# First four value blocks of the gMLP layer computed side by side in four PSUM banks, feature row by feature row; x loaded in eight pieces

## The chip, the cores and the metric

The kernel runs on one core of a Trainium2 chip. Its time is that of one execution on the device, in microseconds (us); lower is better. The engines named below are TensorE (PE; its weight loads are listed as PEld), VectorE (DVE), ScalarE (ACT), GpSimd (POOL) and SyncE (SP), which here only issues DMA loads and stores.

## What is computed

One inference step of a two-layer decoder trunk on 320 tokens at once: 256 of a prompt and 8 x 8 of a sample group. Model width is 1024. Layer 0 mixes tokens with a gated MLP over chunks of 128, layer 1 with an mLSTM; each is followed by a gated MLP with a causal convolution. The change lies in the first matrix product of layer 0, `x @ w_in`, and in what stands around it:

```python
h = rmsnorm(x, norm_mix_g[0])
h = jax.nn.gelu(h @ w_in)                 # 1024 -> 4096
u, v = jnp.split(h, 2, axis=-1)           # 2048 each
v = (v - mu) * rsqrt(var + EPS) * ln_g + ln_b
mixed = einsum('gts,bnsgd->bntgd', tril(w_s), v) + b_s
x = x + (u * mixed) @ w_out
```

## The kernel before

**Layout.** x is kept transposed: `xT` holds 8 feature rows (KD) of 128 features by T = 320 tokens. Weights lie in memory in blocks of 128 output features; a block of `a_win` is 128 x 8 x 128 floats, 512 KB: 8 feature rows of 64 KB. Blocks 0 to 15 give u, blocks 16 to 31 give v; the v blocks come first.

**Precision.** Every f32 product is made of three fast ones. `norm_block` (L163, L164) writes x times the norm's gain as a high half `xh` (ACT) and a low half `xl` (DVE); `prefetch` does the same with weights: `wh` (ACT, L124) and `wl` (DVE, L125). `chunk` then issues, for each feature row k, wh.xh, wh.xl and wl.xh into one PSUM accumulator: 3 matmuls of 128 x 128 by 320 columns a row, 24 a block. The root mean square itself is not applied to x: it enters later, by token, as the scale `rc` of the gelu, or as the row `rb`.

**Queues of weights.** `weights` writes the list of loads for the whole kernel, in the order of use. `prefetch(n, m)` issues loads on SP up to entry n and splits up to entry m. Four `raw` buffers hold loaded entries: a load waits until the split of the entry four places before it is done. `wh` and `wl` have three buffers each: a split waits until PE has finished with the entry three before. `take` hands the next entry to PE, keeping loads 4 entries and splits 1 entry ahead (AHEAD, SPLIT_AHEAD).

**Order.** All PE instructions keep the order in which the program writes them (`pin`). The other engines' queues are ordered by the framework's scheduler when the kernel is built, by priority and by the time at which it reckons each instruction ready; each queue then runs strictly in that order, waiting where it must. Buffers of a pool are handed out by the same scheduler.

**The start.** `run` issues ten warm-up matmuls of `ones` into a PSUM bank `pw`, then loads the first 16 columns of `vecs`, and in four steps two feature rows of x (320 KB) and one entry of weights, with `norm_block` and the weight split behind each. The first block (16) is listed in pieces of 2, 2 and 4 feature rows, the second (17) in two of 4, the others whole. `ident` and the rest of `vecs` are loaded last.

**Layer A.** In the first loop of `layer_a`, over the 16 v blocks, `block` makes one block in one of three `pm` banks of PSUM, DVE copies it to SBUF (`vT`, L289), and one loop pass later `v_nat` turns it by three PE transposes to tokens by features, into banks `pvt`. Four blocks share three `pvt` banks; after the fourth, ACT takes the gelu of each with scale `rc` (L269) and DVE its statistics (L270). Between the blocks stand, each at a fixed loop pass: the squares of x (`square_block`, b = 1: ACT squares, DVE adds to `acc`), `norm_cols` (b = 3: six small matmuls into a bank `pc`; then `ms` on DVE, L193, and `rc` on POOL, L196), `load_ws` (b = 3: loads of the spatial weights, masked by `trit` on POOL, L251), `norm_row` (b = 5: `dg`, `pb`, `rb`) and `row_sums` (b = 10). `pw`, `pvt`, `pc`, `pb` and others share the five `pa` banks; PSUM has eight banks in all.

A second loop makes the u blocks, and what follows in the kernel is not touched by the change.

Of the kernel before, what the change touches and what calls it, by code (L numbers as in the profile page):

```python
# [10 lines left out]
F32 = mybir.dt.float32  # L11
# [5 lines left out]
P = 128  # L17
# [3 lines left out]
T = TP + NB * NS  # L21
D = 1024
KD = D // P
# [10 lines left out]
V_MIX, V_FFN, V_FIN, V_GN, V_LG, V_LB, V_CB, V_FB, V_FW, V_CW = 0, 16, 32, 40, 56, 72, 88, 104, 148, 280  # L34
# [3 lines left out]
class Net:  # L38
# [19 lines left out]
    def weights(self):  # L58

        I = self.I  # L60
        q = []

        def add(w, b, *groups, k0=0):
            for kn in groups:
                q.append((w, b, k0, kn))
                k0 += kn

        add(I["a_win"], 16, 2, 2, 4)
        add(I["a_win"], 17, 4, 4)
        for b in [*range(18, 32), *range(16)]:  # L70
            add(I["a_win"], b, 8)
        for b in range(KD):
            add(I["a_wo"], b, 8, 8)

        def ffn(l):
            for b in range(2 * KF):
                add(I["f_up"][l], b, 8)
            for b in range(KD):
                add(I["f_dn"][l], b, 8, 7, 7)

        ffn(0)
        add(I["b_wg"], 0, 8)
        for h in range(NH):
            for r in range(6):
                if (h, r) == (NH - 1, 4):
                    for b in (0, 1):
                        add(I["b_wo"], b, 6, k0=8)
                add(I["b_win"], 6 * h + r, 8)
                for b in self.EARLY_OUT.get((h, r), ()):
                    add(I["b_wo"], b, 8)  # L90
        for b in range(KD):
            if b < 2:
                add(I["b_wo"], b, 2, k0=14)
            else:
                add(I["b_wo"], b, 8, k0=8)
        ffn(1)
        self.wq = q
        self.loaded, self.halved, self.used = [], [], 0
# [37 lines left out]
    def chunk(self, ps, rhs, first, last):  # L136
        (wh, wl), kn = self.take()
        for k in range(kn):
            xh, xl = rhs(k)
            self.mm(ps[:, :T], wh[:, k, :], xh, first and k == 0, False)  # L140
            self.mm(ps[:, :T], wh[:, k, :], xl, False, False)
            self.mm(ps[:, :T], wl[:, k, :], xh, False, last and k == kn - 1)

    def block(self, kt, rhs):

        ps = self.psm.tile([P, 512], F32, tag="pm", name="pm")
        done = 0
        while done < kt:
            kn = self.wq[self.used][3]
            self.chunk(ps, lambda k: rhs(done + k), done == 0, done + kn == kt)  # L150
            done += kn
        return ps
# [75 lines left out]
    def layer_a(self):  # L228
        nc, tc, I, O = self.nc, self.tc, self.I, self.O
        with tc.tile_pool(name="ya", bufs=1) as yp, tc.tile_pool(name="la", bufs=1) as lp:  # L230
# [13 lines left out]
            def load_ws():  # L244
                nc.sync.dma_start(ws, I["a_ws"])
                nc.sync.dma_start(trit, I["trit"])
                nc.gpsimd.memset(wss[:64], 0.0)
                nc.sync.dma_start(wss[64:], I["a_wss"])
                nc.sync.dma_start(bdt[64:], I["bdt"])
                nc.sync.dma_start(bs, I["a_bs"].to_broadcast([P, NH, P]))  # L250
                nc.gpsimd.tensor_tensor(ws, ws, trit.unsqueeze(1).to_broadcast([P, NH, P]), op=MULT)  # L251
                nc.gpsimd.tensor_tensor(wss[64:], wss[64:], bdt[64:].unsqueeze(1).to_broadcast([64, NH, 64]), op=MULT)

            def row_sums():
                for i in range(2):
                    pr = self.psa.tile([P, 512], F32, tag="pa", name="pr")
                    self.mm(pr, self.ones, ws[:, 4 * i:4 * i + 4, :], True, True)
                    nc.scalar.copy(rsum[:, 4 * i:4 * i + 4, :].rearrange("p g t -> p (g t)"), pr)

            def v_nat(b, vT):  # L260
                q, c = b // 4, b % 4
                if c == 0:
                    pvt[q] = [self.psa.tile([P, 512], F32, tag="pa", name="pvt") for _ in range(3)]
                for t in range(3):
                    self.tr(pvt[q][t][:, c * P:(c + 1) * P], self.tokens(vT, t), self.ident)
                if c == 3:
                    for t in range(3):
                        vv = v[:, t, q * 512:(q + 1) * 512]
                        nc.scalar.activation(vv, pvt[q][t], AF.Gelu_apprx_tanh, scale=self.rc[:, t:t + 1])  # L269
                        nc.vector.bn_stats(st[:, t, q, :], vv)  # L270

            prev = None
            for b in range(16):
                ps = self.block(KD, self.x_rhs)
                if b == 1:
                    with tc.issue_after(self.last_split.ins):
                        for m in range(KD):
                            self.square_block(m)
                if b == 3:
                    self.norm_cols()  # L280
                    load_ws()
                if b == 5:
                    self.norm_row()
                if b == 10:
                    row_sums()
                if prev is not None:
                    v_nat(b - 1, prev)
                prev = lp.tile([P, T], F32, tag="vT", name="vT", bufs=2)
                nc.vector.tensor_copy(prev, ps[:, :T])  # L289

            ve = lp.tile([P, 3], F32, name="ve_a")
            rs = lp.tile([P, 3], F32, name="rstd_a")
# [45 lines left out]
            for b in range(16):  # L338
                ps = self.block(KD, self.x_rhs)
# [586 lines left out]
    def run(self):  # L926
        nc, tc, I, O = self.nc, self.tc, self.I, self.O
        with tc.tile_pool(name="const", bufs=1) as cp, tc.tile_pool(name="xp", bufs=1) as xp, \
                tc.tile_pool(name="wraw", bufs=4) as wraw, tc.tile_pool(name="wsp", bufs=3) as wsp, \
                tc.tile_pool(name="tp", bufs=2) as tp, \  # L930
                tc.tile_pool(name="psm", bufs=3, space=bass.MemoryType.PSUM) as psm, \
                tc.tile_pool(name="psa", bufs=5, space=bass.MemoryType.PSUM) as psa:
            self.wraw, self.wsp, self.tp, self.psm, self.psa = wraw, wsp, tp, psm, psa
            self.xT = xp.tile([P, KD, T], F32, name="xT")
            self.xh = xp.tile([P, KD, T], F32R, name="xh")
            self.xl = xp.tile([P, KD, T], F32R, name="xl")
            self.vecs = cp.tile([P, NVEC], F32, name="vecs")
            self.ident = cp.tile([P, P], F32, name="ident")
            self.ones = cp.tile([P, P], F32, name="ones")
            self.mhalf = cp.tile([P, 1], F32, name="mhalf")  # L940
            self.weights()
            nc.vector.memset(self.mhalf, -0.5)
            warm = cp.tile([P, 1], F32, name="warm")
            nc.scalar.activation(warm, self.mhalf, AF.Gelu_apprx_tanh)
            nc.vector.memset(self.ones, 1.0)
            pw = psa.tile([P, 512], F32, tag="pa", name="pw")
            for i in range(10):
                self.mm(pw[:, :P], self.ones, self.ones, True, True)
            nc.sync.dma_start(self.vecs[:, :16], I["vecs"][:, :16])
            for i in range(4):  # L950
                nc.sync.dma_start(self.xT[:, 2 * i:2 * i + 2, :], I["xT"][:, 2 * i:2 * i + 2, :])
                self.prefetch(i + 1, 0)
                for m in (2 * i, 2 * i + 1):
                    self.norm_block(m, V_MIX)
                self.prefetch(i + 1, min(i + 1, 3))
            nc.sync.dma_start(self.ident, I["ident"])
            nc.sync.dma_start(self.vecs[:, 16:], I["vecs"][:, 16:])
            self.layer_a()
            self.ffn(0, V_MIX + 8)
            self.layer_b()  # L960
            self.ffn(1, None)


def _blocks(w, order=None):

    K, N = w.shape
    b = w.reshape(K // P, P, N // P, P).transpose(2, 1, 0, 3)
    return np.ascontiguousarray(b if order is None else b[order])
# [7 lines left out]
def _lay_out(i):  # L976
    a = {}
    x = np.concatenate([i["x_prompt"].reshape(TP, D), i["x_sample"].reshape(NB * NS, D)])
# [2 lines left out]
        [_cols(i[n]) for n in ("norm_mix_g", "norm_ffn_g", "final_norm_g", "b_gn_g", "a_ln_g", "a_ln_b", "b_conv_b", "f_conv_b",  # L981
                               "f_conv_w", "b_conv_w")], axis=1))
    a["a_win"] = _blocks(i["a_w_in"][0])
    a["a_wo"] = _blocks(i["a_w_out"][0])
    ws = i["a_w_s"][0]
    a["a_ws"] = np.ascontiguousarray(ws.transpose(2, 0, 1))
# [13 lines left out]
    w = i["b_w_in"][0]  # L1000
# [63 lines left out]
```

## Time and profile before

| | |
|---|---|
| median of 3 runs | 982.02 us (981.94 to 982.76) |
| the profiled execution | 981.71 us |
| its span, first to last instruction | 980.0 us |
| granted TensorE clock, mean | 0.996 |
| moved by DMA | 154.63 MB, 158 GB/s over the span |

The profile records one execution. Its views list busy time of each engine, the chain of work that ended last, groups of equal instructions, the waits, the DMA transfers and a timeline of each engine. In a timeline row the columns are the start and duration in us, the engine, the line of the kernel, the operation, what it writes and reads, the tile's size and type, and the number of instructions merged; in brackets stand the idle time of that engine just before it and what ended it. Matmuls overlap in the pipeline, so a matmul's recorded duration is longer than the distance to the next one.

### The profile page before, as it was taken

The page shows a single profiled execution, that of the slowest core. Times are in us where ns is not written, and L with a number is a line of the kernel's source. Part 1 is how long each engine was busy: PE and PEld are TensorE (multiplying, and loading weights), DVE is VectorE, ACT ScalarE, POOL GpSimd, SP SyncE. Part 2 cuts the span into 40 slices and gives each one's busy share as a digit, 9 for nine tenths or more (in the row PEclk, how much of TensorE's full clock was granted, in tenths as well). Part 3 has the DMA queues.
Part 4 walks back from the last instruction along what each step waited for, and adds up shares of the span by engine and source line. Part 5 has one row for each costly group of instructions (what it writes and reads, how often), then busy time and mean ns, then how long its engine had stood idle before and what let it go on. Part 6 is the DMA issues. An engine that isn't in the chain of part 4 may idle for free.

```text
span 980.0 us, 17587 instructions
## 1 busy us (share of the span) xinstructions
PE 966.2 (99%) x6695; PEld 959.7 (98%) x6695; DVE 700.6 (71%) x1358; ACT 510.4 (52%) x918; POOL 95.4 (10%) x266
## 2 busy tenths in 40 slices
PE   9999999999999999999999999999999999999996
PEld 8999999999999999999999999999999999999996
DVE  6647985577777764559999988787787777775442
ACT  6437444454544543349676765565555455544332
POOL 0100000010000000013231111111101000000000
PEclk9999999999999999999999999999999999999998
DMA  8535434444444455455565664553364444445541
GB/s 281 199 129 152 131 136 150 150 151 151 151 144 156 143 154 143 153 174 169 167 214 165 202 199 157 173 175 136 129 210 139 152 151 151 151 145 150 154 119 54
DMA packets 55958, 154.63 MB, mean 158 GB/s; under 512 B 6610, under 2 KB 17490, under 8 KB 55874
## 3 DMA queue, kind: packets, MB, share of 16 engines
q1 hardware_dynamic: 55874, 153.51, 48.1%
q8 instruction: 53, 0.87, 0.4%
q14 instruction: 31, 0.25, 0.1%
HBM read 141.55 MB, written 11.94 MB: 157 GB/s over the span
## 4 chain that ended last, share of the span: by engine, by line
PE 83%; issue 10%; DVE 4%; ACT 2%; DMA 1%; SPq 0%; POOL 0%; POOLq 0%; DVEq 0%; ACTq 0%
PE pm L47 75%; PE num L47 2%; PE pcs L47 1%; PE pmix L47 1%; DVE wl L125 1%; DVE bcv L601 1%; PE pvt L50 1%; DMA xT<-in_xT 0%; ACT wh L124 0%; PE pv L50 0%; PE psc L47 0%; PE pCp L47 0%; PE phn L50 0%; DMA C<-in_C 0%; PE pg L47 0%
## 5 line engine op out<-in xcount | busy, mean ns | idle before, releaser
L124 ACT CAST wh<-raw 128x1024 fp32r<-128x1024 f32 (+3 forms) x253 | 257.3, 1018 | 355.0 <-PE pm L47 197.2
L47 PE MATMUL pm<-xh,wh 128*128 128x320 f32 x1344 | 419.3, 312 | 1.0 <-ACT wh L124 1.0
L47 PE MATMUL pm<-xh,wl 128*128 128x320 f32 x1344 | 415.9, 309 | 1.9 <-DVE wl L125 1.7
L47 PE MATMUL pm<-xl,wh 128*128 128x320 f32 x1344 | 415.1, 309 | 0.0
L125 DVE TENSOR_TENSOR wl<-raw,wh 128x1024 fp32r<-128x1024 f32 (+3 forms) x253 | 299.6, 1185 | 117.4 <-ACT wh L124 114.8
L47 PEld LDWEIGHTS pm<-xh,wl 128*128 128x128 f32 x1344 | 252.2, 188 | 3.2 <-DVE wl L125 3.2
L47 PEld LDWEIGHTS pm<-xh,wh 128*128 128x128 f32 x1344 | 252.5, 188 | 1.9 <-ACT wh L124 1.5
L47 PEld LDWEIGHTS pm<-xl,wh 128*128 128x128 f32 x1344 | 252.5, 188 | 0.2
L47 PE MATMUL pm<-yh_f,wh 128*128 128x320 f32 x352 | 109.0, 310 | 0.0
L47 PE MATMUL pm<-yh_f,wl 128*128 128x320 f32 x352 | 108.5, 308 | 0.0
L47 PE MATMUL pm<-yl_f,wh 128*128 128x320 f32 x352 | 108.5, 308 | 0.0
L47 PEld LDWEIGHTS pm<-yl_f,wh 128*128 128x128 f32 x352 | 66.1, 188 | 0.0
L47 PEld LDWEIGHTS pm<-yh_f,wh 128*128 128x128 f32 x352 | 66.1, 188 | 0.0
L47 PEld LDWEIGHTS pm<-yh_f,wl 128*128 128x128 f32 x352 | 66.1, 188 | 0.0
L393 DVE SCALAR_TENSOR_TENSOR fcv<-fpad,vecs,fcv 128x336 f32<-128x336 f32 x88 | 49.6, 566 | 2.1 <-ACT fcv L391 0.7
L216 DVE TENSOR_TENSOR xT<-pm,xT 128x320 f32<-128x320 f32 x40 | 19.5, 490 | 41.9 <-PE pm L47 41.9
L47 PE MATMUL pm<-ylb,wh 128*128 128x320 f32 x128 | 39.9, 312 | 0.5 <-DVE ylb L815 0.4
L47 PE MATMUL pm<-yhb,wh 128*128 128x320 f32 x128 | 40.0, 312 | 0.4 <-ACT yhb L814 0.4
L47 PE MATMUL pm<-yhb,wl 128*128 128x320 f32 x128 | 39.6, 309 | 0.0
L47 PE MATMUL pm<-yh_a,wh 128*128 128x320 f32 x128 | 39.6, 309 | 0.0
L47 PE MATMUL pm<-yh_a,wl 128*128 128x320 f32 x128 | 39.5, 308 | 0.0
L47 PE MATMUL pm<-yl_a,wh 128*128 128x320 f32 x128 | 39.5, 308 | 0.0
(254 smaller groups left out, 1262.6 us busy)
## 6 DMA issues: line engine op xcount, KB each, us to landing
raw<-in_f_up SPq DMA_DIRECT2D x88, 512.0 KB, 3.3
raw<-in_b_win SPq DMA_DIRECT2D x48, 512.0 KB, 3.4
raw<-in_a_win SPq DMA_DIRECT2D x30, 512.0 KB, 3.7
raw<-in_f_dn SPq DMA_DIRECT2D x32, 448.0 KB, 3.3
C<-in_C SPq DMA_DIRECT2D x32, 258.0 KB, 3.7
raw<-in_a_wo SPq DMA_DIRECT2D x16, 512.0 KB, 3.7
raw<-in_f_dn SPq DMA_DIRECT2D x16, 512.0 KB, 3.5
out_Cs<-C SPq DMA_DIRECT2D x32, 256.0 KB, 2.7
```

Of the source, the lines that this page charges most:

```text
L47: self.pin(self.nc.tensor.matmul(out, lhsT, rhs, start=start, stop=stop))
L50: self.pin(self.nc.tensor.transpose(out, in_, ident))
L124: self.last_split = nc.scalar.copy(wh[:, :kn, :], raw[:, :kn, :])
L125: nc.vector.tensor_tensor(wl[:, :kn, :], raw[:, :kn, :], wh[:, :kn, :].bitcast(F32), op=SUB)
L216: self.nc.vector.tensor_tensor(x, ps[:, :T], x, op=ADD)
L393: nc.vector.scalar_tensor_tensor(cv, pd[:, i:i + NC], self.vec(w + i * KF), cv, op0=MULT, op1=ADD)
L601: nc.vector.scalar_tensor_tensor(cv, pd[:, i:i + NC], self.vec(w + 16 * i), cv, op0=MULT, op1=ADD)
```

## The change

- A second copy of the weights of blocks 16 to 19 is laid out by feature row (`a_w4`): entry k is the four blocks' share of feature row k, 256 KB. The weight list begins with these eight entries in place of blocks 16 to 19 (the first two of which came in five pieces).
- `first` makes the four blocks together. It takes three `pm` banks and one `pa` bank, and for each feature row issues 12 matmuls: wh.xh into each of the four banks, then wh.xl, then wl.xh.
- x is loaded one feature row at a time (160 KB). `run` issues the loads of rows 0 to 3, each followed by a weight entry, and the splits of row 0; `first` issues the others, one in each of its passes, and `norm_block` for the row after the one in work.
- The warm-up has eight matmuls instead of ten.
- After `first`, the four accumulators are copied out (`v_copy`); there are four `vT` buffers instead of two. The loop begins at block 4. The squares move from b = 1 to 4, `norm_cols` and `load_ws` from 3 to 6, `norm_row` from 5 to 8, `row_sums` from 10 to 11. The transposes of blocks 0 to 6 are done two, one, two and two at passes 4, 5, 6 and 7; from pass 8 on one block behind, as before.

```diff
--- before.py
+++ after.py
@@ -65,9 +65,9 @@
                 q.append((w, b, k0, kn))
                 k0 += kn
 
-        add(I["a_win"], 16, 2, 2, 4)
-        add(I["a_win"], 17, 4, 4)
-        for b in [*range(18, 32), *range(16)]:
+        for k in range(KD):
+            add(I["a_w4"], k, 4)
+        for b in [*range(20, 32), *range(16)]:
             add(I["a_win"], b, 8)
         for b in range(KD):
             add(I["a_wo"], b, 8, 8)
@@ -141,6 +141,25 @@
             self.mm(ps[:, :T], wh[:, k, :], xl, False, False)
             self.mm(ps[:, :T], wl[:, k, :], xh, False, last and k == kn - 1)
 
+    def load_x(self, k):
+        self.nc.sync.dma_start(self.xT[:, k, :], self.I["xT"][:, k, :])
+
+    def first(self):
+
+        ps = [self.psm.tile([P, 512], F32, tag="pm", name="pm") for _ in range(3)]
+        ps.append(self.psa.tile([P, 512], F32, tag="pa", name="pm"))
+        for k in range(KD):
+            if k + 4 < KD:
+                self.load_x(k + 4)
+            if k + 1 < KD:
+                self.norm_block(k + 1, V_MIX)
+            (wh, wl), _ = self.take()
+            xh, xl = self.x_rhs(k)
+            for w, x, a, z in ((wh, xh, k == 0, False), (wh, xl, False, False), (wl, xh, False, k == KD - 1)):
+                for j in range(4):
+                    self.mm(ps[j][:, :T], w[:, j, :], x, a, z)
+        return ps
+
     def block(self, kt, rhs):
 
         ps = self.psm.tile([P, 512], F32, tag="pm", name="pm")
@@ -269,24 +288,29 @@
                         nc.scalar.activation(vv, pvt[q][t], AF.Gelu_apprx_tanh, scale=self.rc[:, t:t + 1])
                         nc.vector.bn_stats(st[:, t, q, :], vv)
 
-            prev = None
-            for b in range(16):
+            def v_copy(ps):
+                vT = lp.tile([P, T], F32, tag="vT", name="vT", bufs=4)
+                nc.vector.tensor_copy(vT, ps[:, :T])
+                return vT
+
+            vTs = {b: v_copy(ps) for b, ps in enumerate(self.first())}
+            for b in range(4, 16):
                 ps = self.block(KD, self.x_rhs)
-                if b == 1:
+                if b == 4:
                     with tc.issue_after(self.last_split.ins):
                         for m in range(KD):
                             self.square_block(m)
-                if b == 3:
+                if b == 6:
                     self.norm_cols()
                     load_ws()
-                if b == 5:
+                if b == 8:
                     self.norm_row()
-                if b == 10:
+                if b == 11:
                     row_sums()
-                if prev is not None:
-                    v_nat(b - 1, prev)
-                prev = lp.tile([P, T], F32, tag="vT", name="vT", bufs=2)
-                nc.vector.tensor_copy(prev, ps[:, :T])
+                for m in {4: (0, 1), 5: (2,), 6: (3, 4), 7: (5, 6)}.get(b, (b - 1,)):
+                    v_nat(m, vTs.pop(m))
+                vTs[b] = v_copy(ps)
+            prev = vTs.pop(15)
 
             ve = lp.tile([P, 3], F32, name="ve_a")
             rs = lp.tile([P, 3], F32, name="rstd_a")
@@ -944,15 +968,15 @@
             nc.scalar.activation(warm, self.mhalf, AF.Gelu_apprx_tanh)
             nc.vector.memset(self.ones, 1.0)
             pw = psa.tile([P, 512], F32, tag="pa", name="pw")
-            for i in range(10):
+            for i in range(8):
                 self.mm(pw[:, :P], self.ones, self.ones, True, True)
             nc.sync.dma_start(self.vecs[:, :16], I["vecs"][:, :16])
-            for i in range(4):
-                nc.sync.dma_start(self.xT[:, 2 * i:2 * i + 2, :], I["xT"][:, 2 * i:2 * i + 2, :])
-                self.prefetch(i + 1, 0)
-                for m in (2 * i, 2 * i + 1):
-                    self.norm_block(m, V_MIX)
-                self.prefetch(i + 1, min(i + 1, 3))
+            for k in range(4):
+                self.load_x(k)
+                self.prefetch(k + 1, 0)
+                if k == 0:
+                    self.norm_block(0, V_MIX)
+                    self.prefetch(1, 1)
             nc.sync.dma_start(self.ident, I["ident"])
             nc.sync.dma_start(self.vecs[:, 16:], I["vecs"][:, 16:])
             self.layer_a()
@@ -981,6 +1005,7 @@
         [_cols(i[n]) for n in ("norm_mix_g", "norm_ffn_g", "final_norm_g", "b_gn_g", "a_ln_g", "a_ln_b", "b_conv_b", "f_conv_b",
                                "f_conv_w", "b_conv_w")], axis=1))
     a["a_win"] = _blocks(i["a_w_in"][0])
+    a["a_w4"] = np.ascontiguousarray(a["a_win"][16:20].transpose(2, 1, 0, 3))
     a["a_wo"] = _blocks(i["a_w_out"][0])
     ws = i["a_w_s"][0]
     a["a_ws"] = np.ascontiguousarray(ws.transpose(2, 0, 1))
```

## The prediction

> **What bounds the kernel now.** I read the page first, then busy time by stretch, then the chain of waits in order of time, then the engines' own timelines up to 35 us.
>
> ```profile
> span 980.0 us, 17587 instructions
> PE 966.2 (99%) x6695; PEld 959.7 (98%) x6695; DVE 700.6 (71%) x1358; ACT 510.4 (52%) x918; POOL 95.4 (10%) x266
> ```
>
> ```profile
> 1.00:10.33 9.33, 7.88 (x34) 6.43 (x35) 4.50 (x11) 6.08 (x13) 0.32 (x1) 1.00 0.84 280
> 10.33:120.00 109.67, 109.67 (x765) 108.36 (x766) 79.72 (x140) 58.71 (x86) 6.74 (x4) 1.00 0.54 175
> ```
>
> In the second fence the columns are the stretch, its length, then busy time of PE, PEld, DVE, ACT and POOL, the granted clock, the DMA share and GB/s. TensorE works without a gap from 10.33 us through the whole of layer A; only before 10.33 does it stand still. So whatever the change does is decided on PE's own timeline: what it saves ahead of 10.33, less every new gap.
>
> ```profile
> 3.14 4.86 DMA xT<-in_xT
> ...
> 9.64 0.65 DVE wl L125
> ...
> 10.33 5.25 PE pm L47 x34
> 15.58 0.33 PE pvt L50 x3
> 15.91 3.52 PE pm L47 x24
> 19.43 0.33 PE pvt L50 x3
> 19.76 3.51 PE pm L47 x24
> 23.27 0.56 PE pc L47 x6
> ```
>
> This is the chain of waits in order of time. The start hangs on the load of x and the splits behind it; after 10.33 everything on the chain is PE. A block of 24 matmuls takes 3.51 us, 0.146 each, and a value block's three transposes 0.33. From 10.33 to 23.27 PE issues 82 of the first four blocks' 96 matmuls, so 14 were done before. Without the two groups of transposes the four blocks end at 23.27 - 0.66 = 22.61 us: the number to compare with.
>
> ```profile
> 1.16 4.64 PE L47 MATMUL pw<-ones 128*128 128x128 f32 x20 [1.16 <-DVE ones L945]
> 5.65 0.43 PE L47 MATMUL pm<-xh,wh 128*128 128x320 f32 x1
> 5.92 0.31 PE L47 MATMUL pm<-xl,wh 128*128 128x320 f32 x1
> ```
>
> On PE's timeline the warm-up ends at 5.80 and the first real matmul starts at 5.65. After an idle time the second matmul comes 0.27 after the first instead of 0.146: each restart costs another 0.12. Fourteen matmuls are 2.05 us of work, spread over 4.68 us (5.65 to 10.33): about 2.6 us are lost in gaps, and this is the most the change can take away, beyond what an earlier first matmul brings.
>
> **The front, with feature rows.** A row now gives PE 12 matmuls, 12 x 0.146 = 1.75 us, for 160 KB of x and 256 KB of weights. When these land I take from the first uses in the profile.
>
> ```profile
> 4.29 1.01 ACT L163 ACTIVATE xh<-xT,vecs 128x320 fp32r<-128x320 f32 x2 [1.99 <-DMA xT<-in_xT]
> ...
> 6.30 1.02 ACT L163 ACTIVATE xh<-xT,vecs 128x320 fp32r<-128x320 f32 x2 [0.70 <-DMA xT<-in_xT]
> ...
> 8.03 1.01 ACT L163 ACTIVATE xh<-xT,vecs 128x320 fp32r<-128x320 f32 x2 [0.42 <-DMA xT<-in_xT]
> 8.95 0.60 ACT L124 CAST wh<-raw 128x512 fp32r<-128x512 f32 x1
> ...
> 11.73 0.62 ACT L124 CAST wh<-raw 128x512 fp32r<-128x512 f32 x1 [0.53 <-DMA raw<-in_a_win]
> ```
>
> Four of these waited for a load, so they date a sum of KB in the order of issue (8 of vecs, then x and weights in turn; before the last also ident and the rest of vecs): 328 KB at 4.29, 776 at 6.30, 1224 at 8.03, 2540 at 11.73. That is 223, 259 and 356 KB per us. In the new order the sum is 168 after x row 0, 424 after its weights, 840 after row 1, 1256 after row 2, 1672 after row 3. Interpolated, they land at 3.6, 4.7, 6.55, 8.1 and 9.3 us. SP issues them at 0.43 and a little each, eight from 1.26 to about 5.0, as before:
>
> ```profile
> 1.72 0.43 SPq L109 DMA_DIRECT2D raw<-in_a_win  x1
> ```
>
> A row's cast is the 128x512 form, 0.60, so the casts of rows 0 to 3 end near 5.3, 7.15, 8.7 and 9.9. On ACT a row costs 0.60 + about 0.5 (half of the 1.01), and DVE's two splits come to about 1.2 by the rows below; both stay under PE's 1.75. PE starts row 0 at 5.37, row 1 at 7.25 (its cast is just done), and from there each row 1.75 later: 9.0, 10.75, 12.5. The later rows lead by more and more.
>
> x rows 4 to 7 are moved: they now stand on SP behind ident and vecs, and each after the first also behind a weight load that waits for a buffer (four raw buffers; load k+4 waits for row k's split). Load 4 waits for the first split, near 6.0, lands at a sum of 2316 KB, 11.1, and its cast ends at 11.7, needed at 12.5. Load 5 waits for split 1, near 8.0, and lands by its sum, 2732 KB, at 12.3; its cast ends at 12.9, needed at 14.25. Loads 6 and 7 have over 1 us too. So no row starves: 96 x 0.146 + 0.12 behind 5.37 ends the four blocks near 19.6, with 0.1 lost before row 1. Gain: 22.61 - 19.6 = **3.0 us**. Bounds: row 0's 424 KB lie between 328 KB (4.29) and 776 KB (6.30), so the gain lies between 3.4 and 1.4; I keep the interpolated 4.7, which is nearer the first. The Trainium skill, "DMA: Bandwidth & Descriptors", section Bandwidth, asks for transfers of 1 MiB and more and counts a fixed 2.0 us for each; were the eight x loads to pay it one behind another it would eat the gain, but the loads above, of 128 to 320 KB, overlap at 223 to 356 KB per us. Two warm-up calls fewer (8 x 0.464 from 1.16 end at 4.87) leave PE free in time; leaving ten would have held row 0 until 5.65 or so.
>
> **Two new waits.** First, the four accumulators take all three pm banks. Block 4 of the loop cannot start until DVE has copied accumulator 0 out (v_copy, line 289 before).
>
> ```profile
> 12.09 0.49 DVE L289 COPY vT<-pm 128x320 f32<-128x320 f32 x1 [0.16 <-PE pm L47]
> ```
>
> The groups of instructions in the first 40 us (count, busy, mean ns of one, idle before):
>
> ```profile
> L125 DVE TENSOR_TENSOR wl<-raw,wh 128x1024 fp32r<-128x1024 f32 x8 | 9.8, 1220 | 1.6 <-ACT wh L124 1.5
> L125 DVE TENSOR_TENSOR wl<-raw,wh 128x512 fp32r<-128x512 f32 x3 | 2.1, 689 | 0.0
> L164 DVE SCALAR_TENSOR_TENSOR xl<-xT,vecs,xh 128x320 fp32r<-128x320 f32 x8 | 4.1, 549 | 4.8 <-ACT xh L163 4.8
> L269 ACT ACTIVATE v_a<-pvt,rc 128x512 f32<-128x512 f32 x3 | 1.8, 688 | 0.0
> ```
>
> Before, three banks took turns, and a copy had two whole blocks of cover. Now accumulator 0's last matmul is the fourth from the end, issued 0.58 before PE is free and ending 0.31 after issue; the copy can start 0.25 before PE is free and takes 0.49. PE loses 0.29 and a restart, 0.4, with nothing in DVE's way. A whole split of a later block (1.22) queued ahead makes it 1.6; that split's own wh buffer comes free about one row before, so it falls just there. I take 0.9, between them, since both orders of DVE's queue are open. Queued behind the copy are three more copies and the sums of squares; their users (transposes a block later, norm_cols at b=6) are 3 us off.
>
> Second, at b=6 the order on PE, which is fixed by hand, is: block, norm_cols (six matmuls into pc), v_nat(3), v_nat(4). The last opens three new pvt banks. Of five pa banks, three hold pvt of blocks 0 to 3 until their gelu, one holds pc, one is free. Transpose 1 can take the free bank, transpose 2 that of pc once ms has read it; transpose 3 has none until the first gelu is done, and the gelu needs rc, which this same norm_cols makes. Before, one block lay between norm_cols (b=3) and the gelu (b=4), and another before the new banks (b=5): that cover, two blocks of 3.5 us, is gone. What the chain takes when queues are clear, the next layer's norm_cols shows (PE's timeline, then DVE's and POOL's):
>
> ```profile
> 200.36 0.39 PE L47 MATMUL pm<-xh,wh 128*128 128x320 f32 x1
> ```
>
> ```profile
> 200.53 0.16 DVE L193 TENSOR_SCALAR ms<-pc 128x3 f32<-128x3 f32 x1 [1.01 <-PE pc L47]
> 201.66 0.65 DVE L205 TENSOR_SCALAR dg<-ident,rc 128x128 f32<-128x128 f32 x3 [0.97 <-POOL rc L196]
> ```
>
> ```profile
> 200.78 0.85 POOL L196 TENSOR_TENSOR rc<-ms,mhalf 128x3 f32<-128x3 f32 x1 [53.50 <-DVE ms L193]
> ```
>
> From PE's next instruction (200.36) to the first user of rc (201.66) is 1.30; the gelu is 0.69; with 0.04 to wake PE, 2.03. PE has five transposes to do meanwhile, 0.55. It loses 1.48 and a restart: **1.6 us**. The lower bound is 1.4, since nothing in that chain can be skipped; the upper one is a rival below. Behind the waiting transpose stand block 7 and all of PE.
>
> **What costs nothing.** Nine transposes, the squares (b=1 to 4), norm_row (5 to 8) and row_sums (10 to 11) move in PE's order but keep their count. The squares and sums had ACT and DVE two blocks long; they still have. load_ws moves from b=3 to 6 with its five DMAs on SP, behind the weight loads of three more blocks; row_sums needs ws five blocks later, 19 us. If that cover were short, PE would wait for POOL's product, 2.78.
>
> **The sum**, against the profiled run of 981.71 (span 980.0): -3.0 + 0.9 + 1.6 = -0.5, so 981.2. The runs' median is 0.31 above the profiled run; for it I say **981.5**.
>
> **Rivals.** (1) No wait at the two places, or hardly any: the copy runs first (0.4) and the transposes find a bank. 982.02 - 3.0 + 0.4 = 979.4. For it: pool banks are handed out by the scheduler. Against: seven banks are wanted of five, and PE's order is fixed. 0.12.
>
> (2) Slower: rc sits on POOL behind the masking of ws. It did before:
>
> ```profile
> 23.87 0.16 DVE L193 TENSOR_SCALAR ms<-pc 128x3 f32<-128x3 f32 x1
> ```
>
> ```profile
> 24.96 2.78 POOL L251 TENSOR_TENSOR ws_a<-ws_a,trit 128x1024 f32<-128x1024 f32 x1 [23.64 <-DMA trit<-in_trit]
> 27.70 0.85 POOL L196 TENSOR_TENSOR rc<-ms,mhalf 128x3 f32<-128x3 f32 x1
> ```
>
> ms started at 23.87 and rc at 27.70: 3.83 where 0.25 is the clear chain, 3.6 late, for the mask's load. Then it cost nothing; at b=6 PE would pay it all: 982.02 - 0.5 + 3.6 = 985.1. It decides from 0.5 us of lateness, and by 0.2% from 2.5. Against: ms now falls near 32.6 us (19.6 + 0.9 + three blocks, three v_nat and pc), and the mask was done at 27.74. For: the loads move by the same three blocks. 0.18.
>
> (3) The clock. The warm-up's matmuls came 0.232 apart for 128 columns; later, two f32 matmuls of 320 columns take 0.54:
>
> ```profile
> 31.58 0.54 PE pb L47 x2
> ```
>
> Per column that is 1.81 ns against 0.84, a factor of 2.15, though the granted clock reads 1.00. If 3.7 us of warm-up and a gap of 0.5 don't bring the fast pace, and another 4.64 us must pass, PE loses 4.64 x (1 - 1/2.15) = 2.5: 984.0. Against: the second real matmul before was already fast. 0.10. The Trainium skill, "TensorE: Matmul & The Clock Gate", Part 1, puts the change of pace after about 3.4 us of sustained work, in windows that run freely; by that rule eight calls suffice only if a window falls well, and the trace, one execution, agrees that 4.6 us sufficed.
>
> (4) Rows 1 to 3 starve by 0.4 each: 982.02 - 0.5 + 1.2 = 982.7. 0.10.
>
> **Chances.** Forecast 0.50, with its own range 980.6 (copy 0.4, front 3.4) to 983.2 (one of the two at its worst, the other near it). A run of this kernel can be told from no change at about 0.2%, 1.96 us: 980.06 and 983.98. Faster: rival 1 and a tail of the forecast, 0.15. Slower: most of rival 2, over half of 3, a little of 4, 0.23. Same: 0.62. The range, 979.7 to 984.6, leaves out most of rival 1's best and rival 2's worst.
>
> **What would show it.** PE's first real matmul near 5.4 and no gap to 19.6; a gap of 0.3 to 1.5 before the fifth block, released by vT on DVE; a gap of about 1.5 at v_nat(4), near 33 us, released by the gelu on ACT; POOL's rc right behind ms. Gaps between feature rows, PE pitches of 0.27 after 6 us, or rc waiting for ws would prove me wrong; so would unbroken work on PE through 35 us.

## The result, and the profile after

The changed kernel takes 984.53 us (median of 16 runs, 982.8 to 987.7); the kernel before, run beside it, 981.98 (16 runs, 980.85 to 983.93). The ratio is 1.0025, 95% interval 1.0017 to 1.0033: slower by a quarter of a percent, 2.55 us. The profiled execution took 984.56, with a span of 982.8 against 980.0. The changed kernel's runs cover 4.9 us, those of the kernel before 3.1 here, but 5.1 in the 32 runs beside the first four experiments, so a wider spread is not shown.

PE's timeline, cut to the rows where it had to wait and to those that end or restart a stretch (start, duration, then the idle time before the row and what ended it):

```profile
5.53 0.85 PE L47 MATMUL pm<-xh,wh 128*128 128x320 f32 x4 [0.59 <-ACT wh L124]
...
7.77 0.85 PE L47 MATMUL pm<-xh,wh 128*128 128x320 f32 x4 [0.22 <-ACT wh L124]
...
19.60 0.75 PE L47 MATMUL pm<-xh,wl 128*128 128x320 f32 x4
20.59 0.38 PE L47 MATMUL pm<-xh,wh 128*128 128x320 f32 x1 [0.23 <-DVE vT L293]
...
32.79 0.74 PE L50 MATMUL pvt<-ident,vT 128*128 128x128 f32 x5
36.02 0.42 PE L50 MATMUL pvt<-ident,vT 128*128 128x128 f32 x1 [2.49 <-ACT v_a L288]
36.11 0.61 PE L47 MATMUL pm<-xh,wh 128*128 128x320 f32 x1
36.51 0.47 PE L47 MATMUL pm<-xl,wh 128*128 128x320 f32 x1
36.78 0.47 PE L47 MATMUL pm<-xh,wl 128*128 128x320 f32 x1
...
41.26 0.82 PE L50 MATMUL pvt<-ident,vT 128*128 128x128 f32 x6
```

The reader is to see four things. The feature rows run without a gap from 7.77 on; their last four matmuls start at 19.60, so the four blocks end at 19.60 + 4 x 0.146 = 20.18. The fifth block starts at 20.59 instead. Five of the six transposes run at once, the sixth stands until 36.02. And behind it the matmuls come 0.27 apart (36.51, 36.78), not 0.146: block 7 of the loop, from 36.11 to 41.26, takes 5.15 us where such a block takes 3.60. The view of busy time by stretch names the reason (the figure behind the engines' busy times is the granted clock):

```profile
33.00:36.00 3.00, 0.54 (x5) 0.32 (x3) 0.85 (x3) 1.02 (x3) 2.12 (x2) 1.00 0.59 152
36.00:38.00 2.00, 1.98 (x8) 1.98 (x9) 2.00 (x4) 1.13 (x2) 0.00 (x0) 0.53 0.23 45
...
39.00:39.50 0.50, 0.50 (x4) 0.50 (x3) 0.00 (x0) 0.00 (x0) 0.00 (x0) 0.50 0.57 213
39.50:40.00 0.50, 0.50 (x5) 0.50 (x5) 0.00 (x0) 0.00 (x0) 0.00 (x0) 0.96 0.35 131
```

TensorE's clock was cut to half from about 36.0 to 39.45, right after PE had stood still: the 12 matmuls from 36.11 to 39.18 came at that pace, and the next one in part.

What released the sixth transpose is in the chain of waits, in order of time (start, duration, engine and line):

```profile
24.80 5.60 DMA trit<-in_trit
...
30.54 2.44 POOL ws_a L270
32.98 0.07 issue
33.05 1.27 POOL wss_a L271
34.32 0.07 issue
34.39 0.87 POOL rc L215
35.26 0.02 issue
35.28 0.70 ACT v_a L288
```

The mean square was ready in time (`ms` on DVE, before `rc` in the program):

```profile
32.97 0.16 DVE L212 TENSOR_SCALAR ms<-pc 128x3 f32<-128x3 f32 x1
```

`rc` starts 1.42 after `ms`, where 0.25 is the clear chain: 1.17 late, because both masks of the spatial weights stand ahead of it in POOL's queue. The first, `ws_a`, had waited for the load of `trit`, which SP issued at 24.80 behind two weight loads that waited for their buffers. It ended at 32.98, before `ms` was there (33.13), and alone would have cost nothing. The 1.17 are those of the second mask, `wss_a`, which ran from 33.05 to 34.32. In the kernel before, that mask came behind `rc` (27.70):

```profile
28.63 1.29 POOL L252 TENSOR_TENSOR wss_a<-wss_a,bdt 64x512 f32<-64x512 f32 x1
```

So the change has also changed the order of POOL's queue.

**The balance.** Before, the fifth block of the chain would have started at 22.45: on PE's own timeline norm_cols starts at 23.11, and 0.66 of it are transposes. So the front gains 22.45 - 20.18 = 2.27. The copy of accumulator 0 costs 0.41 and a restart of 0.07: 0.48. The six transposes need 0.57 (41.26 to the next matmul at 41.83), so PE would have been free at 33.36 and was at 36.11: 2.75. The slow block costs 5.15 - 3.60 = 1.55. Together -2.27 + 0.48 + 2.75 + 1.55 = +2.5. The first matmul of the mixing stage, well behind all this, moves by just that:

```profile
L47 PE MATMUL pmix<-ws_a,v_a x64: 272/275/328, 92.9 to 142.0; 128*128 128x128 f32 x64
```

It started at 90.4 before.

### The profile page after: what moved, and what is told of

Read it like the earlier page. It is cut to its first block, busy times and chain, and to the rows that moved or that the text cites. A ratio compares the mean times of both kernels' runs of the same rounds, so it can differ in the third digit from the quotient of the medians.

```text
span 982.8 us, 17583 instructions
## 1 busy us (share of the span) xinstructions
PE 966.3 (98%) x6691; PEld 960.3 (98%) x6691; DVE 700.2 (71%) x1359; ACT 512.2 (52%) x919; POOL 94.5 (10%) x266
## 4 chain that ended last, share of the span: by engine, by line
PE 80%; issue 10%; DVE 4%; DMA 2%; ACT 2%; POOL 1%; SPq 0%; POOLq 0%; DVEq 0%; ACTq 0%
PE pm L47 73%; PE num L47 2%; PE pcs L47 1%; PE pmix L47 1%; DVE wl L125 1%; DMA C<-in_C 1%; DVE bcv L625 1%; DMA trit<-in_trit 1%; ACT wh L124 1%; PE pv L50 0%; PE psc L47 0%; DMA raw<-in_a_w 0%; PE pCp L47 0%; PE pvt L50 0%; PE phn L50 0%
## 5 line engine op out<-in xcount | busy, mean ns | idle before, releaser
L124 ACT CAST wh<-raw 128x1024 fp32r<-128x1024 f32 (+2 forms) x254 | 258.0, 1016 | 353.5 <-PE pm L47 190.7
L125 DVE TENSOR_TENSOR wl<-raw,wh 128x1024 fp32r<-128x1024 f32 (+2 forms) x254 | 299.9, 1181 | 120.3 <-ACT wh L124 117.5
```

The source lines that it names most:

```text
L124: self.last_split = nc.scalar.copy(wh[:, :kn, :], raw[:, :kn, :])
L125: nc.vector.tensor_tensor(wl[:, :kn, :], raw[:, :kn, :], wh[:, :kn, :].bitcast(F32), op=SUB)
```

## The experiments

Seven kernels, each timed in five rounds beside the kernel before, which took 982.0 us in both batches.

### rc ahead of the masks

```diff
-                    load_ws()
+                    with tc.issue_after(self.rc_op.ins):
+                        load_ws()
```

`rc_op` is POOL's instruction that makes `rc`; the block orders POOL's instructions behind it and leaves the loads where they were.

> The masks of the spatial weights are held behind rc in POOL's queue; everything else as in the changed kernel. Theory (rival 2 of the prediction: rc queues behind the masks): rc starts 0.25 after ms instead of 1.42, the sixth transpose waits about 1.5 us instead of 2.75. If the slow block after it (13 matmuls 0.267 apart, granted clock 0.50) comes from PE having stood still too long, it may stay fast: 984.5 - 1.2 - 1.55 = 981.8; if 1.5 us of standing still slow the clock as well, 983.3. Against it, the bank alone would hold PE (my forecast's 1.6): then rc first changes the wait by no more than this 1.2. If the masks do not matter at all: 984.5 and rc as late as before.

Measured: 982.04 (980.81 to 984.53), ratio to before 1.0003 (0.9994 to 1.0012). POOL's, ACT's and PE's timelines of the profiled execution:

```profile
33.48 0.85 POOL L215 TENSOR_TENSOR rc<-ms,mhalf 128x3 f32<-128x3 f32 x1 [32.96 <-DVE ms L212]
```

```profile
34.36 1.85 ACT L288 ACTIVATE v_a<-pvt,rc 128x512 f32<-128x512 f32 x3 [0.80 <-POOL rc L215]
```

```profile
35.10 0.33 PE L50 MATMUL pvt<-ident,vT 128*128 128x128 f32 x1 [1.30 <-ACT v_a L288]
35.19 0.39 PE L47 MATMUL pm<-xh,wh 128*128 128x320 f32 x1
35.42 0.31 PE L47 MATMUL pm<-xl,wh 128*128 128x320 f32 x1
```

`ms` started at 33.23 here, `rc` 0.25 later. PE still stands, for 35.19 - 33.62 = 1.57 (the transposes begin at 33.05 and need 0.57): the forecast's 1.6, almost exactly. Its block goes on at 0.15 a matmul; 1.30 of recorded idle time did not bring the clock down in this execution. So POOL's queue accounts for 1.2 of the wait and the banks for 1.6. Whether a wait of 1.6 costs clock in other executions is open. Each run has its mean granted clock. In the profiled executions without a fall it is 0.996 or 0.997 (it is half at the very end of every one), and a fall of 3.4 us takes 0.0017 off. Five of the 12 runs here have 0.995 (982.3 to 984.5). That is not far from the share of the kernel before, which has no such wait (18 of 56 runs with 0.995 or less); of the changed kernel's 16 runs it is 15.

### Block 4's transposes one pass later

```diff
-                for m in {4: (0, 1), 5: (2,), 6: (3, 4), 7: (5, 6)}.get(b, (b - 1,)):
+                for m in {4: (0, 1), 5: (2,), 6: (3,), 7: (4, 5), 8: (6, 7)}.get(b, (b - 1,)):
```

> Only the order of the transposes changes: block 4's go from loop pass 6 to pass 7, block 6's from 7 to 8; rc stays behind the masks on POOL. Theory (PE stands still because three new banks are wanted before the first gelu): no wait at the transposes, no slow block, 984.5 - 2.75 - 1.55 = 980.2, which is faster than before by 1.8 us: the front's gain (2.27) less the wait for the copy of accumulator 0 (0.48). Rival (the late rc holds PE wherever the transposes stand): a wait of 1 to 2 us moves to pass 7 or 8 and the time stays above 982.

Measured: 979.6 (978.76 to 981.9), ratio 0.9974 (0.9965 to 0.9984): faster than both kernels. On PE's timeline the six transposes at pass 7 follow their block with nothing in front of them,

```profile
37.06 0.82 PE L50 MATMUL pvt<-ident,vT 128*128 128x128 f32 x6
```

although `rc` on POOL is as late as in the changed kernel (`ms` at 33.35):

```profile
34.81 0.86 POOL L215 TENSOR_TENSOR rc<-ms,mhalf 128x3 f32<-128x3 f32 x1
```

The demand for three banks one pass too early is thus the cause of the wait and of the slow block behind it; `rc`'s place on POOL only sets the size. The rival, that a late `rc` holds PE wherever the transposes stand, falls.

### PE kept busy while it waits

```diff
                 for t in range(3):
+                    if b == 4 and t == 2:
+                        fill = self.psm.tile([P, 512], F32, tag="pm", name="fill")
+                        for i in range(16):
+                            self.mm(fill[:, :T], self.xh[:, 0, :P], self.xh[:, 0, :], True, True)
```

> The changed kernel with 16 matmuls whose result nobody reads (2.34 us) put on PE just ahead of the transpose that waits, so that PE stands still for only some 0.4 us; nothing is left out. Theory (the clock is taken back because PE stood still): the block after it runs at 0.146 a matmul, granted clock 1.00, and the kernel is 1.5 us faster for doing more: 983.0. Rival (the slow stretch comes from what runs beside it, the gelus, the statistics or the loads): the block still takes about 5.0 us and the time stays at 984.5.

Measured: 982.19 (981.76 to 984.31), ratio 1.0003 (0.9993 to 1.0014). With 16 matmuls more, the kernel is 2.3 us faster than the changed one.

```profile
33.28 2.58 PE L47 MATMUL fill<-xh 128*128 128x320 f32 x16
...
36.16 0.33 PE L50 MATMUL pvt<-ident,vT 128*128 128x128 f32 x1 [0.29 <-ACT v_a L292]
36.24 0.39 PE L47 MATMUL pm<-xh,wh 128*128 128x320 f32 x1
36.47 0.30 PE L47 MATMUL pm<-xl,wh 128*128 128x320 f32 x1
```

The sixth transpose comes as late as in the changed kernel (36.16 against 36.02), with the same gelus, statistics and loads beside it, and the block behind it runs at full pace. So it is the standing still that takes the clock away. The single runs agree: the mean granted clock is 0.996 or 0.997 in all 11 here, and 0.993 to 0.995 in 15 of the changed kernel's 16. The gain is larger than the 1.5 expected, and the two profiles show where the rest lies. The mixing stage starts at 91.5 here and at 92.9 in the changed kernel: 1.4 is the clock's. About 1.05 more lies in layer 1, where PE waits 0.69 for a weight split just before 476 us here, 1.74 just before 478.3 us in the changed kernel and 1.14 before the change. Neither edit touches that stage, and why this wait differs is open.

### Two accumulators in pa banks

```diff
-        ps = [self.psm.tile([P, 512], F32, tag="pm", name="pm") for _ in range(3)]
-        ps.append(self.psa.tile([P, 512], F32, tag="pa", name="pm"))
+        ps = [self.psm.tile([P, 512], F32, tag="pm", name="pm") for _ in range(2)]
+        ps += [self.psa.tile([P, 512], F32, tag="pa", name="pm") for _ in range(2)]
```

> The transposes as in e2, and two of the four accumulators in pa banks instead of one, so that one pm bank is free when the fifth block starts. Theory (the fifth block waits for the copy of accumulator 0): the gap of 0.48 near 20 us goes, 980.2 - 0.5 = 979.7. Rival (the gap has another cause, such as the split of the fifth block's weights or its load): time as e2.

The lines shown come on top of e2's edit.

Measured: 979.52 (978.62 to 980.96), ratio 0.9976 (0.9967 to 0.9986): no difference from e2 that the interval, a tenth of a percent either way, could show. Its profiled execution (980.72) lost time elsewhere, at the start:

```profile
5.63 1.43 PE L47 MATMUL pm<-xh,wh 128*128 128x320 f32 x4 [0.69 <-ACT wh L124]
6.86 1.27 PE L47 MATMUL pm<-xl,wh 128*128 128x320 f32 x4
7.93 1.27 PE L47 MATMUL pm<-xh,wl 128*128 128x320 f32 x4
8.99 1.23 PE L47 MATMUL pm<-xh,wh 128*128 128x320 f32 x4
10.06 0.75 PE L47 MATMUL pm<-xl,wh 128*128 128x320 f32 x4
```

Four matmuls in 1.06 (6.86 to 7.93, 7.93 to 8.99) are the half pace; the 16 from 5.63 to 10.06 take 4.43 instead of 2.46 (16 x 0.146 and a restart). In the profiles of e1, e2 and e3 only the first four were slowed (0.82 to 0.92 us, where the changed kernel took 0.68). With the four blocks ending so late, the fifth block's start says little here. It can be judged in e7 below, which has the same banks:

```profile
19.69 0.75 PE L47 MATMUL pm<-xh,wl 128*128 128x320 f32 x4
20.27 0.31 PE L47 MATMUL pm<-xh,wh 128*128 128x320 f32 x1
```

The last group of the rows starts at 19.69 and the fifth block 0.58 later, four times 0.146, with no wait. The gap by the copy is gone with a bank free; its 0.48 is too small to be seen in the times.

### Ten and twelve warm-ups

```diff
-            for i in range(8):
+            for i in range(10):
```

> e4 with ten warm-up matmuls instead of eight. In the profile of e4 PE stood still for 0.69 us after the warm-up and then ran the first 16 matmuls or so 0.267 apart, to about 9.8 us, although all runs after a warm-up of ten (before) started at the fast pace. Theory (eight calls leave the clock to chance, rival 3 of the prediction): with ten the first row runs at 0.146, the upper runs of e4 (980.7 to 981.0) vanish and the median comes to 979.3 to 979.6. Rival (the two calls saved are worth their 0.93 us because PE is wanted earlier): 979.9 or more.

The line shown comes on top of e4's edit.

Measured: 979.35 (978.72 to 980.97), ratio 0.9975 (0.9966 to 0.9983). The median is where the first theory put it, but the interval (978.7 to 980.3 us) holds the rival's 979.9 too. One of the 11 runs still took 980.97, and it is the profiled one. Its first row ran at full pace, and it lost its time at the fifth block instead, whose weights came late; PE's row, and ACT's:

```profile
21.86 0.41 PE L47 MATMUL pm<-xh,wl 128*128 128x320 f32 x1 [0.70 <-DVE wl L125]
```

```profile
19.50 2.15 ACT L124 CAST wh<-raw 128x1024 fp32r<-128x1024 f32 x2 [4.07 <-DMA raw<-in_a_win]
```

So time is lost at the front in two ways from one execution to the next, by a slow clock and by a late load, and ten warm-ups are not shown to be better than eight, only not worse.

With `range(12)`:

> e4 with twelve warm-ups, which end near 6.7 us. Theory (row 1's loads, in use from 7.8 to 8.1 us, set the pace of the start, not row 0): row 0 begins 1.0 later than with ten, ends near 8.4, and the whole loses only 0.3 to 0.5: 979.8. Rival (every moment before the first matmul counts): 1.0 slower than e5, 980.5.

Measured: 980.03 (978.81 to 982.12), ratio 0.9977 (0.9967 to 0.9986). The median lies between the two expectations, and the interval (978.8 to 980.6 us) holds both. In the profile the four blocks end at 20.87, 0.6 later than in e5's (20.24), which lies between the two as well: inconclusive.

### x in four loads again

On e5:

```diff
-        self.nc.sync.dma_start(self.xT[:, k, :], self.I["xT"][:, k, :])
+        if k % 2 == 0:
+            self.nc.sync.dma_start(self.xT[:, k:k + 2, :], self.I["xT"][:, k:k + 2, :])
```

> e5 with x in four loads of two feature rows, as before the change (the order of the rest is kept; row 0 now needs 584 KB in place of 424, row 1 the same 840). Theory (row 1's 840 KB set the pace): row 0 starts 0.5 to 0.7 later, row 1 at the same time, and the kernel keeps e5's time within 0.3. Rival (my prediction's reading, in which each row's own landing counts from row 0 on): 0.7 slower than e5.

Measured: 979.61 (979.04 to 981.85), ratio 0.9976 (0.9966 to 0.9986), as e5. The interval, a tenth of a percent either way, would not tell the rival's 0.7 us; the profile decides:

```profile
6.09 0.85 PE L47 MATMUL pm<-xh,wh 128*128 128x320 f32 x4 [0.32 <-ACT wh L124]
6.78 0.75 PE L47 MATMUL pm<-xl,wh 128*128 128x320 f32 x4
7.37 0.75 PE L47 MATMUL pm<-xh,wl 128*128 128x320 f32 x4
7.96 0.75 PE L47 MATMUL pm<-xh,wh 128*128 128x320 f32 x4
```

Row 0 starts 0.65 later than e5's (6.09 against 5.44), and row 1 follows it at 7.96 without a gap, 0.14 behind e5's 7.82 and within the 7.75 to 8.15 at which row 1 started with eight loads in the changed kernel, e1, e2, e3 and e5. Splitting x finer let row 0 start earlier only to wait for row 1. The eight loads are worth nothing that these runs can show.

## Why the prediction was wrong

The median lies in the stated range, at its upper end, but the sign is not the forecast's: I gave "slower" 0.23. Two steps failed. The late `rc` was left out of the sum, which made the wait at the transposes 2.75 instead of 1.6, and what a wait does to the clock was put at nothing, where it cost 1.55. By its steps:

**The front: right mechanism, mis-sized.** 3.0 was forecast, 2.27 came, within the bounds of 1.4 and 3.4. Row 0 started at 5.53 instead of 5.37. Row 1 started at 7.77 instead of 7.25: its cast waited for the weights to 7.10, where my interpolated landing of the sum of 840 KB was 6.55. Together with the restart this is the 0.6 by which the four blocks ended late, 20.18 against 19.6. The other 0.16 is a reading: I took the end before, 22.61, from the chain of waits, whose pieces begin where the one before ended; PE's own timeline has 22.45. Row 1 is the one row that starved, by 0.37; of rival 4 a third came true.

**The copy: right, at its lower bound.** 0.48 against 0.9, with 0.4 as the price when DVE is free. DVE was free:

```profile
19.95 1.68 DVE L293 COPY vT<-pm 128x320 f32<-128x320 f32 x4 [0.40 <-PE pm L47]
21.55 1.22 DVE L125 TENSOR_TENSOR wl<-raw,wh 128x1024 fp32r<-128x1024 f32 x1
```

It had stood idle for 0.40 ahead of the four copies, and the split of a later block, which I feared in front of them, came behind them.

**The transposes: right in place and in the clear price, wrong in what stood on POOL.** Exactly one transpose waited, for the first gelu, as worked out from the banks, and where `rc` is clear the wait is 1.57 (e1) against 1.48 and a restart. In the kernel itself it was 2.75. The failing step is the one that put POOL's queue aside as a rival of 0.18 and gave it no term in the sum. I argued that the mask had been done by 27.74 and `ms` would fall near 32.6; `ms` did come at 32.97, but the mask moved along, from 24.96 to 30.54, since its load stands behind the weight loads of later passes on SP. Rival 2 named the right queue but the wrong instruction: its mask moved by 5.6 us where `ms` moved by 9.1, and was done in time, so the 3.6 did not come. The 1.17 that came is the second mask's, which I had not priced because it stood behind `rc` in the profile of before. I took that order of the queue over into a kernel in which it is another.

**The clock: the step that was missing.** I priced a wait by its length alone. The 1.55 behind it, from matmuls 0.267 apart instead of 0.146, is the largest part of the error: without it the balance is about +1.0, and with the clear chain's 1.57 in place of 2.75 as well it is -0.2. Rival 3 had the mechanism, at the start, where it was not seen in the changed kernel's profile but in e4's; I did not ask what a wait of 1.6, or of 2.75, would do to it in mid-kernel. The Trainium skill, "TensorE: Matmul & The Clock Gate", warns in its section "Why this matters for your kernels" of idle gaps above about 3 us between bursts; by that rule this gap was harmless. The traces differ: 2.49 recorded as idle brought half the clock in the changed kernel, and 1.30 (e1) and 0.29 (e3) did not. The slow stretch of 3.4 us agrees with the window of about 3.4 us that the Trainium skill, "TensorE: Matmul & The Clock Gate", gives in Part 1.

**The sum.** -2.27 + 0.48 + 2.75 + 1.55 = +2.5 stands against -3.0 + 0.9 + 1.6 = -0.5. Of the 3.0 between them the clock is 1.55, the longer wait 1.15 and the front 0.73, and the copy gives back 0.42. With the transposes one pass later the first two terms alone are left, -1.8, and e2's median is 2.4 us below that of the kernel before. Its profile starts the mixing stage 1.4 earlier than before (89.0 against 90.4), since its own front ended later than the changed kernel's; 0.46 more lies in the wait in layer 1, 0.68 against 1.14, outside the change.

## What to carry to other kernels

When work is moved past a stage that frees buffers, count the buffers alive at each point of the fixed order: a tile wanted one pass early cost more than the whole front had gained, and moving it back one pass turned a loss of 0.25% into a gain of 0.26%. Price a wait on TensorE with what it does to the clock, and look in the profile of before for what stands around the releasing instruction in its queue, ahead of it or just behind, even where it costs nothing yet: the order can be another in the changed kernel. Where two pieces must both land before work can run through, loading the first one finer moves the gap instead of closing it.

## What the hardware showed that was not expected

- A gap of 2.5 us in the middle of dense matmul work halved TensorE's clock for 3.4 us in the profiled execution; filling it with 16 useless matmuls avoided this, in the profile and by the mean granted clock in all 11 runs.
- At the start of the kernel the column of the granted clock is no guide: in e4 it reads 1.00 from 5.5 to 10 us while the matmuls come 0.267 apart (the row's columns are those explained in the prediction).

```profile
8.00:9.00 1.00, 1.00 (x6) 1.00 (x5) 0.70 (x2) 0.88 (x3) 0.00 (x0) 1.00 1.04 357
```

- In these rows a wait costs 0.07 to 0.12 more than itself: the second matmul after it starts 0.22 to 0.27 behind the first instead of 0.146. The same 0.23 stands behind transposes without a wait (24.75 to 24.98 in the changed kernel), so the wait is not its only cause.
